# Choice of experts on one core: one-hot work for four heads at once, key rows for eight tokens, and fewer score and row buffers

## The chip, the cores and the metric

The kernel runs on one core of one Trainium2 chip. The metric is device time in microseconds (us) of one execution. In the profile PE is TensorE's matrix multiplication, PEld its weight load, DVE VectorE, ACT ScalarE, POOL GpSimd and SP the engine whose queue issues most DMAs.

## What is computed

One layer of a generator over 1024 latent tokens of width 1024: a mixer (state-space scan and a convolution group, with an output projection), then a retrieval of experts (PEER), then a final norm. The change lies in the retrieval. Each token has 8 heads. A head has two scores against 128 keys each; of each the 16 best are kept, the 16 best of their sums are chosen, and these give 16 of 16,384 experts with softmax gates:

```python
s = jnp.einsum("thpd,hpkd->thpk", q, sub_keys).astype(jnp.float32)
sv, si = lax.top_k(s, PEER_TOPK)
cand = sv[:, :, 0, :, None] + sv[:, :, 1, None, :]
best, flat = lax.top_k(cand.reshape(t, PEER_HEADS, PEER_TOPK * PEER_TOPK), PEER_TOPK)
i1 = jnp.take_along_axis(si[:, :, 0], flat // PEER_TOPK, axis=-1)
i2 = jnp.take_along_axis(si[:, :, 1], flat % PEER_TOPK, axis=-1)
experts = (i1 * N_KEYS + i2).reshape(t, PEER_HEADS * PEER_TOPK)
gates = jax.nn.softmax(best, axis=-1).reshape(t, PEER_HEADS * PEER_TOPK).astype(h.dtype)
act = jax.nn.gelu(jnp.einsum("pd,ped->pe", xb, u_tab[eb]), approximate=False)
out = jnp.einsum("pe,ped->pd", gb * act, v_tab[eb])
```

## The kernel before

**Stages.** The first 700 us or so are the mixer. Then comes the choice of experts for blocks 0 to 6 (a block is 128 tokens, one a partition). In the last stage the experts' work for blocks 0 to 4 is done densely (all 128 groups of 128 experts, L996 and L1443 to L1445, weighted by a gate matrix), while the experts of blocks 5 to 7 are fetched row by row by indirect DMAs (L1286) and worked off on DVE (L1311, L1323); the choice for block 7 runs within this stage, two heads at a time, paced by the matrix work (`advance`, L1357).

**One block's choice** is the generator `select` (L1022), with `nh` heads at once: 8 in the choice stage, 2 for block 7. For each head and each of its two scores DVE finds the 16 best values and their positions with five instructions (`top16`, L1030): values go to `v`, positions to `ix`. `ix` is read as float (L1057), the first key's position is scaled by 128 (L1058), and `stair` (L1037) forms the 50 candidate sums that can be among the best 16: the values on DVE, the key numbers on POOL (L1062), which reads `ixf`, the same memory as `ix`. A second `top16` over the candidates gives `best` and `pos` (L1080). Then the key number of each chosen place is looked up by one-hot work on DVE, head by head (L1084 to L1095): compare the position with a list of candidate positions, `lex` (L1089), multiply by the key numbers (L1091), sum (L1077, in `place`). The first 8 places need only 20 candidates, the other 8 all 50, so a head has two comparisons, two products and two sums over 8 x 20 = 160 and 8 x 50 = 400 elements. The sums of a head are put off until after the next head's products (`pend`). Last come the exponentials and the division (L1097 to L1105).

**The order is written out** by a clock. At each `yield` of `select` a cost is handed to `tick` (L1126), which adds it up and, per 1.0 of cost, takes one step of the oldest waiting work in `fill`, and, per 1.75, one step of `ahead`, the scores of coming blocks. A score phase (the first `top16`s) has 40 yields of 0.4, the rest of a block 19.2 of cost; a block has 35.2.

- `ahead` is `scores` (L1137). A score of a head pair (`score`, L949) is eight matmuls in four steps on TensorE, each record in the trace being half a matmul, and its eviction by ScalarE to a tile `s` comes with the next step (L959). `while len(SC) > 2` (L1143) holds the next one back while three scores lie ready. The scores of block 7 are made in between in blocks 1 and 2 and go to memory. After the scores, `prepare` (L1000) begins the last stage's matrix work.
- `fill` holds the gate matrices of blocks 0 to 4 (`gate_matrix`, L1174), four tokens a step, 32 steps with work and six more. `second` (L1208) builds on DVE a one-hot matrix `ob` of the second key, in 2-byte type, 512 elements a partition (L1211), and ScalarE scales it by the gates to `o2` (L1214); a step later `first` (L1217) builds on DVE `o1`, the first key's, in 4-byte type (L1219); a step later TensorE multiplies them (L1197); a step later ScalarE stores the product (L1204).

DVE, ScalarE and TensorE execute in this written order, each on its own. `tp2` (L1115) holds the tiles of the choice stage; a tile's `bufs` is how many copies take turns. `put` (L1169) gives the tiles of expert numbers `ef` and gates `gt`.

Of the kernel before, what the change touches and what calls it, by code (L numbers as in the profile page):

```python
# [8 lines left out]
F32 = mybir.dt.float32  # L9
F32R = mybir.dt.float32r  # L10
BF16 = mybir.dt.bfloat16
I32 = mybir.dt.int32
U32 = mybir.dt.uint32
AF = mybir.ActivationFunctionType
# [15 lines left out]
NH = 8  # L30
# [42 lines left out]
def layer_kernel(ctx, tc, A, dbg=None):  # L73
# [690 lines left out]
    def natural(blocks, ps, tp, name):  # L764

        for z, k4 in [(z, k4) for z in blocks for k4 in range(2)]:
# [3 lines left out]
            hn = tp.tile([P, 4, P], F32, name=name)  # L770
# [251 lines left out]
    def select(z, tp, nh, scores, put):  # L1022
# [23 lines left out]
        for h0 in range(0, NH, nh):  # L1046
# [20 lines left out]
            best = tp.tile([P, nh, TOPK], F32, name="best", bufs=1)  # L1067
            pos = tp.tile([P, nh, TOPK], U32, name="pos", bufs=1)
            posf = tp.tile([P, nh, TOPK], F32, name="posf", bufs=1)
            ef, gt = put(z, h0)  # L1070
            pend = []

            def place(n):
                while len(pend) > n:
                    q, oh = pend.pop(0)
                    for i, o in enumerate(oh):
                        nc.vector.tensor_reduce(ef[:, q, i * 8:i * 8 + 8], o, axis=mybir.AxisListType.X, op=OP.add)  # L1077

            for q2 in range(0, nh, 2):
# [3 lines left out]
                nc.vector.tensor_copy(posf[:, q2:q2 + 2], pos[:, q2:q2 + 2])  # L1083
                for q in (q2, q2 + 1):  # L1084
                    oh = tp.tile([P, 8, NUP + NCAND], F32, name="oh").rearrange("p a b -> p (a b)")
                    oh = [o.rearrange("p (a b) -> p a b", a=8) for o in (oh[:, :8 * NUP], oh[:, 8 * NUP:])]
                    for i, o in enumerate(oh):
                        sh = [P, 8, NCAND if i else NUP]
                        nc.vector.tensor_tensor(o, posf[:, q, i * 8:i * 8 + 8, None].to_broadcast(sh),  # L1089
                                                lex[:, None, :sh[2]].to_broadcast(sh), op=OP.is_equal)  # L1090
                        nc.vector.tensor_tensor(o, o, cand[:, 1, q, None, :sh[2]].to_broadcast(sh), op=OP.mult)  # L1091
                    pend.append((q, oh))
                    yield 0.7
                    place(nh // 8)
                    yield 0.7  # L1095
            eb = tp.tile([P, nh, TOPK], F32, name="eb", bufs=1)
            nc.vector.tensor_tensor(eb, best, best[:, :, 0:1].to_broadcast([P, nh, TOPK]), op=OP.subtract)  # L1097
            nc.scalar.activation(eb, eb, AF.Exp)
            yield 0.2
            place(0)  # L1100
            yield 0.9
# [12 lines left out]
    with ExitStack() as st:  # L1114
        tp2 = st.enter_context(tc.tile_pool(name="tp2", bufs=2))  # L1115
        spl = st.enter_context(tc.tile_pool(name="spl", bufs=4))
# [20 lines left out]
        def scores():  # L1137
# [3 lines left out]
            for z in range(NS):  # L1141
                for hh in range(4):
                    while len(SC) > 2:  # L1143
                        yield
# [486 lines left out]
```

## Time and profile before

| | us |
|---|---|
| median of three runs | 3053.84 |
| lowest, highest | 3052.66, 3054.78 |
| the profiled execution, its own time | 3052.06 |
| its span in the trace | 3050.3 |

Times are read from the trace of the profiled execution. A start is counted from the start of the span. The time between the starts of two instructions of one engine is what the first costs there when the engine doesn't wait; its length can be more, as the next may begin before it ends. In a row, `oh<-posf,lex 128x400` means the tile written, the tiles read, and partitions by elements; `x2` means two instructions shown as one. `[1.32 <-ACT s L959]` is idle time before the instruction and what ended it.

### The profile page before, as it was taken

Reading aid. Unit: us, or ns where it says so; the run is one execution under the profiler, and the core shown is the slowest. Engines: PE = TensorE matmul, PEld = TensorE weight load, DVE = VectorE, ACT = ScalarE, POOL = GpSimd, SP = SyncE. Lnnn points to the kernel's source line nnn. Section 1 sums busy time; section 2 is a strip of 40 time slices with the busy share of each in tenths; the row PEclk is TensorE's granted clock in tenths of the full one; section 3 lists DMA queues with packets and bytes.
Section 4 is the critical chain, followed back from the end, with each engine's and each line's share of the span. In section 5 each row is a group of like instructions: output and inputs, shape, how many; then the busy total and the mean of one; then the engine's idle time right before and its main releaser. Section 6 shows DMA issues by size and latency. Waiting matters only on the chain.

```text
span 3050.3 us, 41960 instructions
## 1 busy us (share of the span) xinstructions
PE 2836.3 (93%) x15129; PEld 2391.2 (78%) x15129; DVE 2570.6 (84%) x5084; ACT 1060.9 (35%) x2026; POOL 1326.0 (43%) x1043
## 2 busy tenths in 40 slices
PE   7999899998888876999999999999999999999996
PEld 3777698764555556898888998998998898998995
DVE  4898756659999999889989998888998888888886
ACT  3224333333667664332222222222222322322222
POOL 0212343420000002666566656566666566666650
PEclk8999899999999987999999999999999999999998
DMA  6211256250221235888889999998998998999993
GB/s 214 61 36 42 86 165 213 77 189 15 118 107 63 111 125 192 308 312 301 311 297 361 324 346 343 326 340 320 337 344 317 334 357 318 336 342 318 328 326 119
DMA packets 334545, 722.68 MB, mean 237 GB/s; under 512 B 24560, under 2 KB 167168, under 8 KB 333056
## 3 DMA queue, kind: packets, MB, share of 16 engines
q0 software_dynamic: 112176, 408.47, 37.1%
q1 hardware_dynamic: 222160, 311.53, 29.5%
q8 instruction: 119, 1.95, 0.2%
q14 instruction: 90, 0.74, 0.1%
HBM read 658.56 MB, written 61.35 MB: 236 GB/s over the span
## 4 chain that ended last, share of the span: by engine, by line
PE 58%; DVE 27%; issue 5%; DMA 5%; POOL 3%; ACT 2%; SPq 0%; DVEq 0%; POOLq 0%; ACTq 0%
PE pa L996 22%; PE pv L1444 8%; PE pv L1445 8%; PE pv L1443 8%; PE pa L68 4%; DVE o L1219 3%; DVE cfm L413 2%; DVE oh L1091 2%; DVE ob L1211 2%; POOL gr L1286 2%; DVE oh L1089 2%; DVE gr L1311 1%; DVE ef L1077 1%; PE pq L953 1%; PE po L68 1%
## 5 line engine op out<-in xcount | busy, mean ns | idle before, releaser
L1286 POOL DMA_INDIRECT gr<-in_peer_v_dram,idx x384 | 546.8, 1424 | 309.3 <-DVE h2T L1323 209.7
L1286 POOL DMA_INDIRECT gr<-in_peer_u_dram,idx x384 | 524.1, 1365 | 361.4 <-DVE gr L1311 249.2
L1444 PE MATMUL pv<-vl,wh 128*128 128x512 f32 x1240 | 495.5, 400 | 19.5 <-DVE vl L61 17.3
L1323 DVE SCALAR_TENSOR_TENSOR h2T<-gr,wv,h2T 128x1024 f32<-128x1024 f32 x381 | 488.5, 1282 | 13.6 <-DMA gr<-in_peer_v_dram,idx 6.0
L1443 PE MATMUL pv<-vh,wl 128*128 128x512 f32 x1240 | 493.4, 398 | 1.5 <-ACT vh L60 1.4
L1445 PE MATMUL pv<-vh,wh 128*128 128x512 f32 x1240 | 493.6, 398 | 0.0
L1311 DVE SCALAR_TENSOR_TENSOR gr<-gr,h2T 128x1024 f32<-128x1024 f32 x384 | 455.5, 1220 | 23.5 <-DMA gr<-in_peer_u_dram,idx 23.3
L60 ACT ACTIVATE vh<-v 128x512 fp32r<-128x512 f32 x256 | 161.5, 632 | 656.1 <-PE pv L1445 616.7
L996 PE MATMUL pa<-hh,ul 128*128 128x320 f32 x2000 | 335.0, 310 | 3.2 <-DVE ul L988 3.2
L996 PE MATMUL pa<-hh,uh 128*128 128x320 f32 x2000 | 334.6, 309 | 0.0
L996 PE MATMUL pa<-hl,uh 128*128 128x320 f32 x2000 | 334.0, 309 | 0.3 <-ACT ga L1406 0.3
L996 PEld LDWEIGHTS pa<-hl,uh 128*128 128x128 f32 x2000 | 304.8, 188 | 3.3 <-ACT ga L1406 0.6
L996 PEld LDWEIGHTS pa<-hh,ul 128*128 128x128 f32 x2000 | 304.2, 188 | 3.7 <-DVE ul L988 3.7
L996 PEld LDWEIGHTS pa<-hh,uh 128*128 128x128 f32 x2000 | 304.4, 188 | 0.0
L1444 PEld LDWEIGHTS pv<-vl,wh 128*128 128x128 f32 x1240 | 235.0, 190 | 80.0 <-DVE vl L61 22.8
L1406 ACT ACTIVATE ga<-pa 128x320 f32<-128x320 f32 x252 | 109.2, 436 | 525.2 <-PE pa L996 507.1
L1443 PEld LDWEIGHTS pv<-vh,wl 128*128 128x128 f32 x1240 | 235.1, 190 | 57.8 <-ACT vh L60 2.4
L61 DVE TENSOR_TENSOR vl<-v,vh 128x512 fp32r<-128x512 f32 x256 | 176.4, 690 | 122.5 <-ACT vh L60 114.9
L1445 PEld LDWEIGHTS pv<-vh,wh 128*128 128x128 f32 x1240 | 235.3, 190 | 56.1
L1197 PEld LDWEIGHTS pg<-o,o 128*128 128x128 f32 x1280 | 174.1, 207 | 128.2 <-ACT o L1214 109.2
L1197 PE MATMUL pg<-o,o 128*128 128x128 f32 x1280 | 188.0, 297 | 75.7 <-ACT o L1214 67.3
L1214 ACT ACTIVATE o<-ob,tr 128x128 f32<-128x128 bf16 x640 | 209.4, 399 | 96.4 <-DVE ob L1211 94.4
(344 smaller groups left out, 4241.5 us busy)
## 6 DMA issues: line engine op xcount, KB each, us to landing
v<-in_peer_v_dram SPq DMA_DIRECT2D x256, 256.0 KB
u<-in_peer_ut_dram SPq DMA_DIRECT2D x87, 512.0 KB
g_dram<-stg SPq DMA_DIRECT2D x10, 4096.0 KB
gm<-g_dram SPq DMA_DIRECT2D x64, 640.0 KB
h2T<-in_peer_ut_dram SPq DMA_DIRECT2D x41, 512.0 KB
ld<-in_ada_w_dram SPq DMA_DIRECT2D x24, 512.0 KB
w<-in_w_in_t_dram SPq DMA_DIRECT2D x21, 512.0 KB
raw<-in_ada_w_dram SPq DMA_DIRECT2D x8, 1024.0 KB
```

What stands on the lines that cost most here:

```text
L60: nc.scalar.activation(hi, src, AF.Copy)
L61: (eng or nc.vector).tensor_tensor(lo, src, hi.bitcast(F32), op=OP.subtract)
L68: nc.tensor.matmul(out, a(k)[i], b(k)[j], start=start and t == 0 and k == 0, stop=stop and t == 2 and k == n - 1)
L996: nc.tensor.matmul(pa[half], x[:, k], y[:, k, half * TH:half * TH + TH], start=t == 0 and k == 0, stop=t == 2 and k == KD - 1)
L1197: nc.tensor.matmul(pg[:, j], o2[:, j], o1[:, j], start=True, stop=True)
L1214: nc.scalar.activation(o2[:, j], ob[:, :, j], AF.Copy, scale=tr[:, 1, t4 * 4 + j:t4 * 4 + j + 1])
L1286: nc.gpsimd.indirect_dma_start(out=g, out_offset=None, in_=A[t], in_offset=bass.IndirectOffsetOnAxis(ap=idx[:, b, e:e + 1], axis=0))
L1311: nc.vector.scalar_tensor_tensor(g, g, 1.0, h2, op0=OP.mult, op1=OP.mult, accum_out=act[:, e:e + 1])
L1323: nc.vector.scalar_tensor_tensor(ac, g, wv[:, e:e + 1], ac, op0=OP.mult, op1=OP.add)
L1443: nc.tensor.matmul(Out.pv[t], wl[:, sl], self.vh, start=i == 0, stop=False)
L1444: nc.tensor.matmul(Out.pv[t], wh[:, sl], self.vl, start=False, stop=False)
L1445: nc.tensor.matmul(Out.pv[t], wh[:, sl], self.vh, start=False, stop=i == GE - 1)
```

## The change

Nine edits, all in the choice of experts:

1. The one-hot work is done after the second `top16` of all heads, for `w` = 4 heads at once (2 for block 7): comparison, product and sum over 4 x 8 x 20 = 640 or 4 x 8 x 50 = 1600 elements, with a yield after each, and one buffer `oh`.
2. All positions of a block are cast to float in one instruction, not per two heads.
3. `best` and the exponentials lie in `v`, `pos` and its float form in `ix`, in place of tiles of their own.
4. The exponentials are formed ahead of the one-hot work.
5. `ob` is built for eight tokens at once, in every second step, with 2 larger buffers instead of 3; `o2` has 3 buffers instead of 4.
6. `o1` is built for eight tokens at once, in every second step.
7. The score tiles have 3 buffers instead of 4, and `scores` holds the next one back while two lie ready.
8. `ef` and `gt` have 2 buffers instead of 3.
9. A tile of another helper that shares the name `o1` gets the same size.

```diff
--- before.py
+++ after.py
@@ -767,7 +767,7 @@
             pt = ps.tile([P, 4, P], F32, name="pt")
             for a in range(4):
                 nc.tensor.transpose(pt[:, a], h2T[:, k4 * 4 + a, z * P:(z + 1) * P], ident)
-            hn = tp.tile([P, 4, P], F32, name=name)
+            hn = tp.tile([P, 8 if name == "o1" else 4, P], F32, name=name)[:, :4]
             nc.scalar.activation(hn, pt, AF.Copy)
             nc.sync.dma_start(h2n_dram[(z - ND) * P:(z - ND + 1) * P, k4 * 512:k4 * 512 + 512],
                               hn.rearrange("p k t -> p (k t)"))
@@ -1064,41 +1064,31 @@
             yield 0.5
             stair(nc.vector, v, cand[:, 0], SUMS[3:], SUMS[:3])
             yield 0.5
-            best = tp.tile([P, nh, TOPK], F32, name="best", bufs=1)
-            pos = tp.tile([P, nh, TOPK], U32, name="pos", bufs=1)
-            posf = tp.tile([P, nh, TOPK], F32, name="posf", bufs=1)
+            best, eb = v[:, :, 0], v[:, :, 1]
+            pos, posf = ix[:, :, 0], ixf[:, :, 1]
             ef, gt = put(z, h0)
-            pend = []
-
-            def place(n):
-                while len(pend) > n:
-                    q, oh = pend.pop(0)
-                    for i, o in enumerate(oh):
-                        nc.vector.tensor_reduce(ef[:, q, i * 8:i * 8 + 8], o, axis=mybir.AxisListType.X, op=OP.add)
-
             for q2 in range(0, nh, 2):
                 for n in together([top16(best[:, q], pos[:, q], cand[:, 0, q], tp.tile([P, NCAND], F32, name="c2", bufs=2))
                                    for q in (q2, q2 + 1)]):
                     yield 0.12 * n
-                nc.vector.tensor_copy(posf[:, q2:q2 + 2], pos[:, q2:q2 + 2])
-                for q in (q2, q2 + 1):
-                    oh = tp.tile([P, 8, NUP + NCAND], F32, name="oh").rearrange("p a b -> p (a b)")
-                    oh = [o.rearrange("p (a b) -> p a b", a=8) for o in (oh[:, :8 * NUP], oh[:, 8 * NUP:])]
-                    for i, o in enumerate(oh):
-                        sh = [P, 8, NCAND if i else NUP]
-                        nc.vector.tensor_tensor(o, posf[:, q, i * 8:i * 8 + 8, None].to_broadcast(sh),
-                                                lex[:, None, :sh[2]].to_broadcast(sh), op=OP.is_equal)
-                        nc.vector.tensor_tensor(o, o, cand[:, 1, q, None, :sh[2]].to_broadcast(sh), op=OP.mult)
-                    pend.append((q, oh))
-                    yield 0.7
-                    place(nh // 8)
-                    yield 0.7
-            eb = tp.tile([P, nh, TOPK], F32, name="eb", bufs=1)
+            nc.vector.tensor_copy(posf, pos)
             nc.vector.tensor_tensor(eb, best, best[:, :, 0:1].to_broadcast([P, nh, TOPK]), op=OP.subtract)
             nc.scalar.activation(eb, eb, AF.Exp)
-            yield 0.2
-            place(0)
-            yield 0.9
+            yield 1.1
+            w = min(nh, 4)
+            for q, i in [(q, i) for q in range(0, nh, w) for i in range(2)]:
+                sh = [P, w, 8, NCAND if i else NUP]
+                oh = tp.tile([P, w * 8 * NCAND], F32, name="oh", bufs=1)[:, :w * 8 * sh[3]]
+                oh = oh.rearrange("p (w a b) -> p w a b", w=w, a=8)
+                nc.vector.tensor_tensor(oh, posf[:, q:q + w, i * 8:i * 8 + 8, None].to_broadcast(sh),
+                                        lex[:, None, None, :sh[3]].to_broadcast(sh), op=OP.is_equal)
+                yield 0.2 * w
+                nc.vector.tensor_tensor(oh, oh, cand[:, 1, q:q + w, None, :sh[3]].to_broadcast(sh), op=OP.mult)
+                yield 0.2 * w
+                nc.vector.tensor_reduce(ef[:, q:q + w, i * 8:i * 8 + 8], oh, axis=mybir.AxisListType.X, op=OP.add)
+                yield 0.3 * w
             sm = tp.tile([P, nh], F32, name="sm")
             nc.vector.tensor_reduce(sm, eb, axis=mybir.AxisListType.X, op=OP.add)
             nc.vector.reciprocal(sm, sm)
@@ -1113,7 +1103,7 @@
     with ExitStack() as st:
         tp2 = st.enter_context(tc.tile_pool(name="tp2", bufs=2))
-        spl = st.enter_context(tc.tile_pool(name="spl", bufs=4))
+        spl = st.enter_context(tc.tile_pool(name="spl", bufs=3))
         gst = st.enter_context(tc.tile_pool(name="gst", bufs=2))
         psT = st.enter_context(tc.tile_pool(name="psT", bufs=2, space=PSUM))
         psG = st.enter_context(tc.tile_pool(name="psG2", bufs=3, space=PSUM))
@@ -1140,7 +1130,7 @@
             extra = [(z, hh) for z in range(NS, NT) for hh in range(4)]
             for z in range(NS):
                 for hh in range(4):
-                    while len(SC) > 2:
+                    while len(SC) > 1:
                         yield
                     yield from begun.pop(0) if begun else score(z, hh)
                     if z and hh % 2 and extra:
@@ -1167,8 +1157,8 @@
         EG = {}
         def put(z, h0):
-            EG[z] = (tp2.tile([P, NH, TOPK], F32, name="ef", bufs=3),
-                     heads(gates[:, z - ND], 0, NH) if z >= ND else tp2.tile([P, NH, TOPK], F32, name="gt", bufs=3))
+            EG[z] = (tp2.tile([P, NH, TOPK], F32, name="ef"),
+                     heads(gates[:, z - ND], 0, NH) if z >= ND else tp2.tile([P, NH, TOPK], F32, name="gt"))
             return EG[z]
         def gate_matrix(z, ef, gt):
@@ -1206,19 +1196,25 @@
                     nc.sync.dma_start(g_dram[z, t4 // 16], stg[0])
             def second(t4):
-                ts = slice(t4 * 4, t4 * 4 + 4)
-                ob = tp2.tile([P, P, 4], BF16, name="ob", bufs=3)
-                nc.vector.tensor_tensor(ob, iotx, tb[:, None, ts].to_broadcast([P, P, 4]), op=OP.is_equal)
-                o2 = tp2.tile([P, 4, P], F32, name="o2", bufs=4)
+                if t4 % 2 == 0:
+                    ts = tb[:, t4 * 4:t4 * 4 + 8].rearrange("p (a b) -> p a b", b=4)
+                    second.ob = tp2.tile([P, 2, P, 4], BF16, name="ob")
+                    nc.vector.tensor_tensor(second.ob, iotx[:, None].to_broadcast([P, 2, P, 4]),
+                                            ts[:, :, None].to_broadcast([P, 2, P, 4]), op=OP.is_equal)
+                o2 = tp2.tile([P, 4, P], F32, name="o2", bufs=3)
                 for j in range(4):
-                    nc.scalar.activation(o2[:, j], ob[:, :, j], AF.Copy, scale=tr[:, 1, t4 * 4 + j:t4 * 4 + j + 1])
+                    nc.scalar.activation(o2[:, j], second.ob[:, t4 % 2, :, j], AF.Copy,
+                                         scale=tr[:, 1, t4 * 4 + j:t4 * 4 + j + 1])
                 return t4, o2
             def first(t4, o2):
-                o1 = tp2.tile([P, 4, P], F32, name="o1")
-                nc.vector.tensor_tensor(o1, iot[:, None].to_broadcast([P, 4, P]),
-                                        tr[:, 0, t4 * 4:t4 * 4 + 4, None].to_broadcast([P, 4, P]), op=OP.is_equal)
-                return t4, o1, o2
+                if t4 % 2 == 0:
+                    first.o1 = tp2.tile([P, 8, P], F32, name="o1")
+                    nc.vector.tensor_tensor(first.o1, iot[:, None].to_broadcast([P, 8, P]),
+                                            tr[:, 0, t4 * 4:t4 * 4 + 8, None].to_broadcast([P, 8, P]), op=OP.is_equal)
+                return t4, first.o1[:, t4 % 2 * 4:t4 % 2 * 4 + 4], o2
             stg = [None]
             got = [None] * 3
```

## Rows read from the trace of the kernel before

**Rows 1.** Stretches: length, us busy (instructions) of PE, PEld, DVE, ACT, POOL; clock; DMA.

```profile
1000.00:1100.00 100.00, 80.30 (x380) 55.78 (x381) 98.07 (x401) 67.86 (x192) 6.10 (x22) 0.90 0.21 90
...
1400.00:1500.00 100.00, 94.20 (x530) 85.64 (x529) 91.36 (x204) 28.70 (x46) 60.96 (x52) 0.98 0.87 310
...
1600.00:1700.00 100.00, 99.92 (x539) 88.69 (x539) 91.33 (x93) 26.21 (x42) 66.75 (x48) 1.00 0.96 353
```

**Rows 2.** Chain of waits from 735 to 1155 us, shares by line.

```profile
by line: DVE o L1219 22.3%; DVE ob L1211 12.5%; DVE oh L1091 8.6%; DVE oh L1089 7.6%; DVE ef L1077 6.7%; DVE ix L1032 5.9%; DVE scr L1033 5.7%; DVE ix L1035 5.6%; DVE v L1031 4.4%; DVE v L1034 4.2%; DVE pos L1035 1.8%; DVE pos L1032 1.8%; D
```

**Rows 3.** Who waited for whom, 700 to 1200 us: us, times, longest.

```profile
ACT o L1214 <- DVE ob L1211: 94.4, 93, 4.9
...
DVE v L1031 <- ACT s L959: 6.0, 4, 2.1
...
PE pv L996 <- DVE ul L988: 2.0, 1, 2.0
```

**Rows 4.** DVE's integer copy of the choices, its line and one of them (start, length).

```profile
L1107 DVE CAST idx<-ef x6: 174/176/221, 1124.4 to 1592.9; 128x32 int32<-128x32 f32 x4, 128x128 int32<-128x128 f32 x2
...
1200.04 0.22 DVE L1107 CAST idx<-ef 128x128 int32<-128x128 f32 x1
```

**Rows 5.** DVE in order of time, one head's one-hot work: start us, length us, operation.

```profile
1106.92 0.33 DVE L1089 TENSOR_TENSOR oh<-posf,lex 128x160 f32<-128x160 f32 x1
1107.28 0.33 DVE L1091 TENSOR_TENSOR oh<-oh,cand 128x160 f32<-128x160 f32 x1
1107.53 0.57 DVE L1089 TENSOR_TENSOR oh<-posf,lex 128x400 f32<-128x400 f32 x1
1108.13 0.57 DVE L1091 TENSOR_TENSOR oh<-oh,cand 128x400 f32<-128x400 f32 x1
1108.62 0.42 DVE L1211 TENSOR_TENSOR ob<-iotx,tb 128x512 bf16<-128x512 bf16 x1
1108.96 0.68 DVE L1219 TENSOR_TENSOR o<-iot,tr 128x512 f32<-128x512 f32 x1
1109.56 0.79 DVE L1077 TENSOR_REDUCE ef<-oh 128x8 f32<-128x160 f32 x2
1110.26 0.41 DVE L1211 TENSOR_TENSOR ob<-iotx,tb 128x512 bf16<-128x512 bf16 x1
```

**Rows 6.** DVE in order of time, a cast of positions and what follows.

```profile
1103.25 0.18 DVE L1083 CAST posf<-pos 128x32 f32<-128x32 uint32 x1
1103.46 0.33 DVE L1089 TENSOR_TENSOR oh<-posf,lex 128x160 f32<-128x160 f32 x1
```

**Rows 7.** DVE in order of time, the waits for scores in blocks 2 and 3.

```profile
827.66 0.49 DVE L1031 MAX8 v<-s 128x8 f32<-128x128 f32 x2 [1.32 <-ACT s L959]
...
915.33 0.49 DVE L1031 MAX8 v<-s 128x8 f32<-128x128 f32 x2 [1.32 <-ACT s L959]
```

**Rows 8.** TensorE in order of time: gate-matrix steps (8 records), a score step (4).

```profile
1055.57 1.13 PE L1197 MATMUL pg<-o,o 128*128 128x128 f32 x8 [0.47 <-ACT o L1214]
1056.53 1.88 PE L953 MATMUL pq<-m,h2T 128*128 128x512 f32 x4
1058.25 1.05 PE L1197 MATMUL pg<-o,o 128*128 128x128 f32 x8
```

**Rows 9.** DVE, the end of block 3's choice and of block 4's score phase.

```profile
970.28 0.28 DVE L1103 TENSOR_REDUCE sm<-eb 128x8 f32<-128x128 f32 x1
...
999.86 0.23 DVE L1058 TENSOR_SCALAR ix<-ix 128x128 f32<-128x128 f32 x1
```

**Rows 10.** POOL and DVE in order of time, around the first search of positions.

```profile
924.59 3.90 POOL L1041 TENSOR_TENSOR cand<-ix 128x64 f32<-128x64 f32 x11 [74.69 <-DVE ix L1058]
...
1080.30 2.49 POOL L1041 TENSOR_TENSOR cand<-ix 128x64 f32<-128x64 f32 x11 [76.45 <-DVE ix L1058]
...
1081.91 0.09 DVE L1032 MATCH_VALUE_LOAD pos<-best,cand 128x8 f32 x1
```

**Rows 11.** ScalarE in order of time, stores of two gate-matrix steps.

```profile
1099.72 0.57 ACT L1204 ACTIVATE stg<-pg 128x512 f32<-128x512 f32 x1
...
1101.38 0.58 ACT L1204 ACTIVATE stg<-pg 128x512 f32<-128x512 f32 x1
```

## The prediction

> **What bounds the kernel now.** I read the busy time by stretches first, because the change touches only the choice of experts and the gate matrices beside it, about a sixth of the span. In that stage VectorE (DVE) is busy 98% of the time, TensorE 80%, ScalarE 68% [rows 1]. A busy share alone doesn't say that an engine sets the end, so the chain of waits comes next: between 735 and 1155 us it runs almost wholly over DVE, and more than half of it lies in the lines that the change rewrites [rows 2]. The waits agree: DVE waited only 6.0 us for a score, while ScalarE waited 94.4 us for DVE's `ob` [rows 3]. At the stage's end TensorE waits for DVE's `ul`, and DVE turns to those right behind the last choice, at 1200.04 us [rows 3, 4]. So DVE time saved in this stage moves everything behind it forward by as much, as long as DVE stays the bound.
>
> **What the larger operations save.** Element counts stay; only fixed costs go. Start to start, a product that needs the comparison in front of it comes 0.36 us after 160 elements and 0.60 after 400, 1.0 ns an element and 0.20 us fixed; where the next instruction needs nothing from the one in front, it is 0.25 and 0.49, so 0.09 fixed [rows 5].
>
> One-hot work: a head takes 1.70 us for four operations and 0.70 for its two sums, 2.40 in all and 19.2 us for eight heads [rows 5]. Afterwards twelve operations do it: 3 x 8 x 8 x 70 = 13,440 elements, 13.4 us, plus twelve fixed parts. In blocks 1 to 5 a gate-matrix operation mostly stands between two of them (0.09 each, 1.1 us); in blocks 0 and 6 mostly not (0.20, 2.4 us). Saved: about 4.6 us in five blocks and 3.4 in two, 30 us. Four casts of positions become one: three times 0.21 us go [rows 6], the one left is 96 elements longer, so 0.5 us a block, 3.5 us.
>
> Gate matrices: 32 `ob` and 32 `o1` a block become 16 and 16, so 160 instructions go in five blocks. `ob` holds DVE 0.34 us and `o1` 0.60 for 512 elements; at 0.5 and 1.0 ns an element 0.08 and 0.09 are fixed [rows 5]. Taken at a little less, 0.075, since two points give the slope only roughly: 12 us. **DVE saves 45 us**, give or take 3 for the fixed parts.
>
> [...] The rows show 0.09 to 0.20 us fixed, because the next instruction starts before the last has ended (the 0.33 us product at 1107.28 is followed at 1107.53) [rows 5]. [...] I take the rows' value.
>
> **What it adds.** First, fewer scores ready. A block's score phase has 40 steps of 0.4, 16 units of the selection's clock; the scores ahead get one step per 1.75 units, and a score takes four steps and a fifth for its eviction. Before, three scores lie ready when a block begins, so only head pair 3 (needed at unit 12) must be made, ready at unit 8.75. Now two lie ready: pair 2 is finished at 8.75, needed at 8, and pair 3 needs ten steps by unit 12, which gives seven; the missing ones are issued at the last moment. In the kernel before, this happens only in blocks 2 and 3, which also make scores of block 7; DVE waited 1.3 us at each of three places (the first and the last of them in [rows 7]). Afterwards seven more places have no slack. Price from below: 7 x 1.3 = 9 us. From above: one step is 1.72 us of TensorE and one gate-matrix step 0.96 [rows 8]; ten steps and about nine gate-matrix steps are 25.8 us, and DVE gets there after 12/16 of a 29.6 us phase [rows 9] less 0.6 saved, at 21.6; with the eviction that is a wait of 4.8 us, six blocks 29, less the 3.9 there already: 25 us. Block 4, whose phase I took, is the shortest, so the others wait less: I take 15, nearer to the lower row.
>
> Second, positions now lie in the buffer of key indices, which POOL still reads. The first search of positions loads its keys at 1081.91; POOL's additions, started at 1080.30, end at 1082.79 [rows 10]. DVE would wait 0.9 us here with everything queued behind it. In other blocks gate-matrix operations come between, but POOL also takes up to 3.90 us [rows 10]. Bounds over seven blocks: 0 and 9 us; I take 4.
>
> At nothing: fewer `ob`, `o2`, `ef` and `gt` buffers. ScalarE's steps follow each other in 1.66 us [rows 11], while DVE needs 29.6 / 16 = 1.85 us a unit, thus a step, in that short phase [rows 9], and `ob` serves two steps, so ScalarE waits less. If TensorE fell two steps behind, three `o2` buffers would stop ScalarE and the score evictions behind it; that is inside the upper bound above. The exponentials move ahead of the one-hot work, which hides them. In the last stage (block 7, two heads at a time) DVE loses 24 instructions, but the work there is TensorE's (94% and later 100% busy [rows 1]): no gain. Each of its four groups has 26 steps instead of 25, so the two further gather buffers come about 4 x 3.9 = 16 us later (100 steps between 1200.04 and 1592.9 [rows 4]); at 6% idle TensorE that is below 1 us.
>
> **The sum:** 45 - 15 - 4 = 26 us less. The profiled execution took 3052.06 us, the median of the runs is 3053.84; 26 off the one is 3026, off the other 3028, and I give 3028. The case's own range: 48 - 9 - 0 = 39 at best, 42 - 25 - 9 = 8 at worst, 3015 to 3046.
>
> **The rivals.** Something below 0.2% (6 us) can't be told from no change.
> - *Forecast, 3028*, chance 0.72.
> - *The score phase becomes TensorE's* (0.11): every score then waits as in the upper bound, and the three-deep `o2` holds ScalarE back as well, some 3 us a block on top. 45 - 25 - 18 = 2 us less: 3052, no change. For it: TensorE is already 80% busy [rows 1], and most of a score is made in that phase. Against it: the three places that had no slack waited 1.3 us only.
> - *`ob` loses its double rate* (0.08): over a third dimension. 512 elements in 2-byte type hold DVE 0.34 us, as many in 4-byte type 0.60 [rows 5]. At one element a step a pair takes 1.02 + 0.08 instead of 0.59, 0.51 us more, 80 times: 41 us on the bound engine. 41 - 26 = 15 us more: 3069, slower. It decides as soon as a pair takes over 0.92 us. For it: nothing in the trace has this shape. Against it: the innermost run of four elements stays as it is. [...]
> - *Fixed costs larger than start to start shows* (0.09): 433 instructions go in seven blocks (36 and 3 in each, and 160), and if each frees all that its duration has above its elements (0.57 us for 400, at 1.0 ns, is 0.17 [rows 5]), 433 x 0.17 = 74 and 74 - 19 = 55 us less: 2999. Against it: DVE starts the next instruction earlier than that. [...]
>
> Faster by over 0.2% means below 3047.7: the forecast and the last rival, 0.81; the forecast's range ends below it. Within 0.2%: 0.11. Slower: 0.08. The range 3010 to 3050 holds the forecast's and some of the second case; left out are the slower case, the large gain and a tail, under 0.2.
>
> **What would show it.** Right: the double `ob` at 0.68 us (not 1.2), the one-hot operations at about 0.8 and 1.8 us, four of each a block; DVE waiting for scores some 20 us in all, mostly at pairs 2 and 3, and up to 1 us a block for POOL; the last choice ending near 1174 instead of 1200, and all behind it shifted by the same. Wrong: waits for scores of over 40 us, TensorE above 95% busy in the stage; or the stage shorter by 26 us and the end not, were the last stage bound by something that doesn't start with it.

## The result and the profile after

The changed kernel takes 3028.69 us, the median of four runs (3025.99 to 3033.13); the kernel before took 3053.25 beside it. The ratio is 0.9924, with a 95% interval of 0.991 to 0.9937: faster by 24.6 us. The forecast was 3028. Its size came out by two misses against each other, and the profile shows both: VectorE (DVE) saved more than forecast, and the start of the last stage gave some of it back.

In the times of the runs, 0.2% is 6 us. Runs of one kernel differ by that much and more, so what follows leans on the traces: when the last choice ends, and when TensorE reaches a certain matmul. The profiled execution took 3029.6 us (before: 3052.06).

First the stretches, as in [rows 1]: length, then busy us and instructions of PE, PEld, DVE, ACT and POOL, the granted clock, the DMA share and GB/s.

```profile
1000.00:1100.00 100.00, 77.29 (x400) 57.98 (x401) 95.84 (x285) 74.42 (x215) 2.53 (x11) 0.91 0.20 85
1400.00:1500.00 100.00, 95.08 (x543) 86.94 (x542) 90.93 (x195) 27.37 (x44) 61.11 (x53) 0.98 0.88 302
```

In the choice stage DVE has 285 instructions in 100 us instead of 401, and its share fell by two points: it now waits. TensorE did not become the bound there (77%).

The chain of waits (710 to 1130 us, shares by line) says so as well; it answers to [rows 2]:

```profile
by line: DVE o L1215 15.4%; PE pq L953 12.1%; PE pg L1187 9.2%; DVE ob L1203 8.4%; DVE oh L1088 7.3%; DVE oh L1085 7.1%; DVE ef L1090 6.4%; DVE ix L1032 5.5%; DVE ix L1035 4.9%; POOL cand L1041 3.8%; DVE v L1031 3.7%; DVE v L1034 3.5%; DVE 
```

TensorE's score and gate-matrix lines are in it with 21% and POOL's with 4%. Before, the lines at the head of the chain were all DVE's.

Next, DVE's groups by line and shape, 690 to 1180 us (count, busy us and mean ns of one, idle time before):

```profile
L1215 DVE TENSOR_TENSOR o<-iot,tr 128x1024 f32<-128x1024 f32 x80 | 97.3, 1216 | 0.0
L1203 DVE TENSOR_TENSOR ob<-iotx,tb 128x1024 bf16<-128x1024 bf16 x80 | 54.3, 679 | 0.0
...
L1085 DVE TENSOR_TENSOR oh<-ix,lex 128x1600 f32<-128x1600 f32 x14 | 26.8, 1917 | 0.1
...
L1075 DVE CAST ix<-ix 128x128 f32<-128x128 uint32 x7 | 1.6, 226 | 0.2
```

The double `ob` lasts 679 ns, where half of it lasted 415 on average before: 0.52 ns for each further element, near the 0.5 of the prediction's estimate, so its rate is what it was. One cast a block is left, 226 ns.

Who waited for whom, 705 to 1168 us, against [rows 3]:

```profile
ACT o L1207 <- DVE ob L1203: 68.8, 53, 3.5
...
DVE v L1031 <- ACT s L959: 17.3, 10, 2.9
...
DVE ix L1032 <- POOL cand L1041: 3.5, 6, 0.8
```

DVE waits for a score at ten places, 17.3 us, and for POOL's key numbers in six blocks, 3.5 us. In the kernel before, from 705 us on, it waited for a score at three places:

```profile
DVE v L1031 <- ACT s L959: 3.9, 3, 1.3
```

The end of the last choice, in order of time, answers to [rows 4, 5]:

```profile
1158.46 0.82 DVE L1085 TENSOR_TENSOR oh<-ix,lex 128x640 f32<-128x640 f32 x1
1159.31 0.82 DVE L1088 TENSOR_TENSOR oh<-oh,cand 128x640 f32<-128x640 f32 x1
1160.17 0.82 DVE L1090 TENSOR_REDUCE ef<-oh 128x32 f32<-128x640 f32 x1
1161.03 1.82 DVE L1085 TENSOR_TENSOR oh<-ix,lex 128x1600 f32<-128x1600 f32 x1
1162.77 1.22 DVE L988 TENSOR_TENSOR ul<-u,uh 128x1024 fp32r<-128x1024 f32 x1
1163.91 1.82 DVE L1088 TENSOR_TENSOR oh<-oh,cand 128x1600 f32<-128x1600 f32 x1
1165.76 1.82 DVE L1090 TENSOR_REDUCE ef<-oh 128x32 f32<-128x1600 f32 x1
...
1168.25 0.22 DVE L1097 CAST idx<-ef 128x128 int32<-128x128 f32 x1
```

Six operations do what 24 did for four heads. The last copy of the choices starts at 1168.25 instead of 1200.04 us: the choice stage is 31.8 us shorter. But TensorE gained less from it. The 190th matmul into `pv`, a fixed point early in the last stage, starts at 1246.90 us after the change and at 1271.46 before, 24.6 earlier, and the last one 23.3 earlier. So some 7 us were lost between the last choice and TensorE's work behind it. The time from the end of the last choice to that 190th matmul is called the handover below: 71.2 us before the change, 78.4 after it.

SP's queue shows where. Before the change (start us, time to the last issue of the group, what is loaded):

```profile
1190.94 0.33 SPq L978 DMA_DIRECT2D u<-in_peer_ut_dram  x1
...
1192.31 5.90 SPq L1385 DMA_DIRECT2D gm<-g_dram  x2
1198.68 7.79 SPq L1428 DMA_DIRECT2D v<-in_peer_v_dram  x5
1206.53 0.42 SPq L978 DMA_DIRECT2D u<-in_peer_ut_dram  x1
```

and after it:

```profile
1164.01 0.33 SPq L978 DMA_DIRECT2D u<-in_peer_ut_dram  x1
...
1168.39 1.99 SPq L1381 DMA_DIRECT2D gm<-g_dram  x2
1170.43 9.78 SPq L1424 DMA_DIRECT2D v<-in_peer_v_dram  x5
1180.26 0.42 SPq L978 DMA_DIRECT2D u<-in_peer_ut_dram  x1
```

The first load of a gate matrix (`gm`) went out 7.9 us ahead of the choice's end; now it goes out 0.1 us ahead, because its memory lies on `v` and `ix`, which the change keeps in use to the end of the choice (the exponentials in `v`, the positions in `ix`); the experiments with tiles of their own, below, bear this out. The `v` and `u` loads stand behind it in the queue. The `u` that left 6.3 us behind the last choice now leaves 11.8 us behind it, and TensorE meets that:

```profile
1183.36 1.34 PE L996 MATMUL pa<-hh,uh 128*128 128x320 f32 x8
1187.44 2.50 PE L996 MATMUL pa<-hl,uh 128*128 128x320 f32 x8 [2.75 <-ACT uh L984]
1189.74 1.82 PE L996 MATMUL pa<-hh,ul 128*128 128x320 f32 x8
1191.40 1.33 PE L996 MATMUL pa<-hh,uh 128*128 128x320 f32 x8
```

It waits 2.75 us for `uh`, and the two groups behind the wait take 2.50 and 1.82 us where others take 1.34. The kernel before has no such gap here. Five of the 7 us lie around this wait, between the 64th and the 127th matmul into `pv`; 1.4 lie ahead of it and 0.8 behind it.

### The profile page after: what moved, and what is told of

It reads as the page before. It is cut to its first block, busy times and chain, and to the rows that moved or that the text cites. A ratio compares the mean times of both kernels' runs of the same rounds, so it can differ in the third digit from the quotient of the medians.

```text
span 3027.8 us, 41488 instructions
## 1 busy us (share of the span) xinstructions
PE 2830.4 (93%) x15129; PEld 2389.9 (79%) x15129; DVE 2525.5 (83%) x4627; ACT 1054.2 (35%) x2026; POOL 1333.3 (44%) x1043
## 4 chain that ended last, share of the span: by engine, by line
PE 62%; DVE 23%; DMA 5%; issue 4%; POOL 3%; ACT 2%; SPq 0%; DVEq 0%; POOLq 0%; ACTq 0%
PE pa L996 23%; PE pv L1440 8%; PE pv L1441 8%; PE pv L1439 8%; DVE cfm L413 3%; PE pq L953 3%; PE pa L68 3%; DVE o L1215 2%; PE po L68 2%; PE pg L1187 1%; DVE gr L1307 1%; DMA gr<-in_peer_u_dram,idx 1%; DVE oh L1085 1%; DVE oh L1088 1%; DVE ob L1203 1%
## 5 line engine op out<-in xcount | busy, mean ns | idle before, releaser
L1041 POOL TENSOR_TENSOR cand<-ix 128x32 f32<-128x32 f32 (+6 forms) x121 | 49.3, 445 | 463.3 <-DVE ix L1058 463.3
L953 PE MATMUL pq<-m,h2T 128*128 128x512 f32 x512 | 238.9, 606 | 0.4 <-DMA m<-m_dram 0.4
```

The source lines that it names most:

```text
L953: nc.tensor.matmul(ps, h2T[:, k, z * P:(z + 1) * P], m[:, k, hh * 512:hh * 512 + 512], start=k == 0, stop=k == KD - 1)
```

## The experiments

Three theories were open. (1) The sum is right term by term: one-hot work, gate matrices, waits for scores. (2) Rivals: a term is worth more or less than its arithmetic says, or one wait only moves to another place. (3) The end of the choice is not passed on in full, because of the queue shown above. The kernel before was run beside each group: 3056.41 us (first four), 3057.0 (next four), 3054.75 (last four). A ratio is to those. A trace shows one execution, and in it the choice stage begins with DVE's first search of a score: at 678.7 us before the change, at 679.2 after it, and anywhere from 676.1 to 683.7 in the traces below. So where two traces are compared, the length of the choice stage counts, from there to the end of the last choice: 521.5 us before the change, 489.3 after it.

### Four tokens again: what the wider rows are worth

```diff
-                if t4 % 2 == 0:
-                    second.ob = tp2.tile([P, 2, P, 4], BF16, name="ob")
...
+                ob = tp2.tile([P, P, 4], BF16, name="ob", bufs=3)
...
-                    first.o1 = tp2.tile([P, 8, P], F32, name="o1")
...
+                o1 = tp2.tile([P, 4, P], F32, name="o1")
```

> The changed kernel with the one-hot rows (ob and o1) built for four tokens again, 160 more instructions on VectorE; all else as changed. By the theory (VectorE sets the stage's pace, and an instruction that is independent of the one in front costs 0.07 to 0.08 us beside its elements) the stage and the whole get 11 to 13 us longer: about 3041 us. Rival 1, the whole fixed part of an instruction's duration counts (0.17 us): 27 us longer, 3056. Rival 2, with so few scores ready TensorE sets the pace of the stage: at most 3 us longer, 3032.

3040.76 us, ratio 0.9954 (0.9942 to 0.9967). The last choice ends 10.8 us later than in the changed kernel:

```profile
1179.08 0.22 DVE L1097 CAST idx<-ef 128x128 int32<-128x128 f32 x1
```

The waits for scores and POOL were 3.4 us shorter and a new one, for a free `o` buffer, 1.8 us, so DVE's work itself grew by 10.8 + 3.4 - 1.8 = 12.4 us. Added up from start to start, `ob` and `o1` alone take 150.7 us instead of 138.7, 12.0 more. The term of 12 us stands.

### Head by head again: what the one-hot work is worth

```diff
-            w = min(nh, 4)
-            for q, i in [(q, i) for q in range(0, nh, w) for i in range(2)]:
...
+            pend = []
...
+            for q in range(nh):
...
+                pend.append((q, oh))
+                yield 0.7
+                place(nh // 8)
+                yield 0.7
+            place(0)
```

> The changed kernel with the one-hot work head by head as before (six operations a head, sums put off by one head), 36 more instructions a block; casts, buffers and scores as changed. Theory: 30 us longer (4.6 us in each of five blocks and 3.4 in two), about 3058 us. Rival 1 (0.17 us for each of 252 instructions): 43 us longer, 3072. Rival 2 (TensorE sets the pace): under 15 us longer, below 3044.

3054.01 us, ratio 0.9997 (0.9989 to 1.0006): without this part the change gains nothing that can be measured. Summed over seven blocks, the work behind the score phase is 31.4 us longer (288.8 against 257.4), and the last choice ends 33 us later:

```profile
1201.32 0.22 DVE L1106 CAST idx<-ef 128x128 int32<-128x128 f32 x1
```

The term of 30 us stands. The time, though, lost only some 22 us (0.9997 - 0.9924, 0.0073 of 3055; against the changed kernel's second runs below, 0.9907, it is 27, and either is uncertain by 5 to 7). TensorE runs 29.6 us behind the changed kernel at 1254 us, and 21.6 at 1640: 8 us came back within the last stage. This stretch of matrix work, the 190th to the 1009th matmul into `pv`, takes 393.6 us in the kernel before, 393.2 in the changed one and 385.0 here; 385 to 387 are also seen in the traces of two further kernels below, 391 to 394 in all others. TensorE's waits in this stretch add up to 11 to 12.5 us in these three traces, at a mean granted clock of 0.99, and to 12 to 16 us in the others, at 0.97 to 0.99. Each of the three is the shortest or second shortest execution of its kernel (here 3050.0 us, of eleven up to 3059.34), so the difference may belong to the execution and not to the edit. What sets it was not found.

### Three scores ready again

This one starts from the kernel with four tokens, whose smaller rows leave memory for a fourth score buffer.

```diff
-        spl = st.enter_context(tc.tile_pool(name="spl", bufs=3))
+        spl = st.enter_context(tc.tile_pool(name="spl", bufs=4))
...
-                    while len(SC) > 1:
+                    while len(SC) > 2:
```

> The kernel of e1 with three scores ready again (four score buffers); to be compared with e1. Theory: VectorE's waits for scores fall from about 17 us to about 4 and the time by as much, 13 us: about 3028 us. Rival: the waits only show that TensorE is full in this stage, so they turn up elsewhere: same as e1, within 3 us.

3028.51 us, ratio 0.9904 (0.989 to 0.9919), so 12.3 us below the kernel it starts from (0.0050 in ratios, 15 us, uncertain by about 6). DVE's waits, 700 to 1170 us, in the kernel it starts from and here:

```profile
DVE v L1031 <- ACT s L959: 17.2, 11, 2.8
...
DVE v L1031 <- ACT s L959: 6.0, 4, 2.1
DVE o L1209 <- PE pg L1187: 2.3, 4, 0.9
```

The waits for scores are the 6.0 us of [rows 3] again. The rival, that the waits move to the gate matrices, falls here but for about half a microsecond (1.8 there); a base further below shows more of it. The choice stage is 10.8 us shorter (490.1 against 500.9) and the handover 2.2. So the fewer score buffers cost 12 to 15 us, for which the forecast had 15.

### Moving the first tiles of the last stage

```diff
         ep2 = st.enter_context(tc.tile_pool(name="ep2", bufs=2, reuse_waits="tile"))
+        for _ in range(2):
+            for n, d, k in (("vh", F32R, 512), ("vl", F32R, 512), ("ga", F32, TD)):
+                ep2.tile([P, k], d, name=n)
```

> The changed kernel; in the last stage other tiles (vh, vl, ga) are put first in their pool, so that the first gate-matrix loads gm no longer lie on the memory of the tiles of the choice (v, ix) that now live to its end. Theory of the handover (the choice ends 31.8 us earlier, but TensorE is only 25.4 us earlier some 50 us later, because gm, v and u loads are issued behind the last choice): gm and v are issued some us before the last choice ends, TensorE has no wait of 2.8 us for u, and 4 to 6 us are gained, about 3024 us. Rival: the loads are bound by the transfers themselves, or other tiles hold them: no change, 3029 within 2 us.

3026.78 us, ratio 0.9905 (0.9889 to 0.9922). It tells nothing of the handover: `gm` came to lie on other tiles that are in use to the end (its load is released by the last copy of the choices), and left at 1168.22 us, as late as in the changed kernel. TensorE stood where it stood in the changed kernel at 1224 us. This is one of the two further kernels in whose trace the matrix work took 385 to 387 us later on; its runs lie between 3016.81 and 3035.53 us, and the traced one took 3017.55.

### The changed kernel again, and `gm` on memory that is free early

```diff
+        for n, d, sh, k in (("vh", F32R, [512], 2), ("gm", F32, [ND * 2, 2, P // 2], 2), ("ga", F32, [TD], 2),
+                            ("vl", F32R, [512], 2), ("act", F32, [P], 2), ("wv", F32, [P], 2), ("v", F32, [512], NV)):
+            for _ in range(k):
+                ep2.tile([P, *sh], d, name=n, bufs=k)
```

The first run has no edit; the second orders the tiles so that the first `gm` should lie on `o1`.

> The changed kernel itself, as the base for e6 to e8 on the same chip: 0.8% below the kernel before, the last choice ending some 32 us earlier and the matrix work of the last stage some 25 us earlier.

3030.99 us, ratio 0.9907 (0.9887 to 0.9928).

> The changed kernel with the last stage's tiles in another order in their pool: the first gate-matrix tile gm now lies on the rows o1, which are free once the gate matrices are done, and the v tiles on ob and o2 (in e4 gm had come to lie on cand, oh, ef and gt, which live to the end too). Theory of the handover: the first gm load no longer waits for VectorE, gm and v are issued 3 to 4 us earlier, TensorE's wait for u is gone, and 3 to 6 us are gained against e5. Rival: other things set the first 50 us of the last stage: no change within 2 us.

3028.76 us, ratio 0.9903 (0.9882 to 0.9925): 2.2 us less, inside the uncertainty. The trace decides. With the choice's last copy at 1170.64, `gm` leaves 3.1 us ahead of its end:

```profile
1167.78 4.22 SPq L1385 DMA_DIRECT2D gm<-g_dram  x2
1172.04 10.28 SPq L1428 DMA_DIRECT2D v<-in_peer_v_dram  x5
```

Yet the handover is 78.4 us, against 78.2 in the changed kernel's second trace, and TensorE waits as long as ever (waits of PE, 1150 to 1230 us):

```profile
PE pa L996 <- ACT uh L984: 3.1, 1, 3.1
```

So `gm`'s wait for the choice alone was not it. In front of `gm` stands the load of the next `u`, which waits until DVE has read the last one (`ul`). DVE does that between operations of the choice, 5.7 us ahead of the choice's end; before the change it was 10.6 us. And behind `gm` the `v` loads still left 1.2 us behind the end.

### Two faster kernels

The first builds only `ob` for eight tokens, and has three scores ready and tiles of its own for the exponentials and positions; the second keeps eight tokens for both, and does the one-hot work for two heads at a time, with three scores ready and tiles of its own for the exponentials and the positions as floats.

```diff
-            best, eb = v[:, :, 0], v[:, :, 1]
-            pos, posf = ix[:, :, 0], ixf[:, :, 1]
+            best = v[:, :, 0]
+            eb = tp.tile([P, nh, TOPK], F32, name="eb", bufs=1) if nh == NH else v[:, :, 1]
+            pos = tp.tile([P, nh, TOPK], U32, name="pos", bufs=1) if nh == NH else ix[:, :, 0]
+            posf = tp.tile([P, nh, TOPK], F32, name="posf", bufs=1) if nh == NH else ixf[:, :, 1]
```

and, in the second alone, where `pos` stays in `ix`:

```diff
-            w = min(nh, 4)
+            w = min(nh, 2)
```

> The changed kernel with o1 for four tokens again (80 more instructions), which frees memory for four score buffers with three scores ready, and for tiles of their own for the exponentials and positions. Theory: + 6 us for o1, - 13 for the waits for scores, - 3.5 for the waits for POOL, - 4 at the handover (gm's first load no longer behind v): 14 us less than e5. Rival (TensorE is full in this stage and takes what the waits give): 0 to 6 us more than e5.

3015.54 us, ratio 0.9873 (0.9853 to 0.9894): 15.5 us below the changed kernel's second runs in medians and 10.4 in ratios, uncertain by about 9. That fits the theory's 14, and the rival, no gain, falls.

> The changed kernel with the one-hot work for two heads at once (24 instead of 12 instructions a block), which frees memory for four score buffers with three scores ready, and for tiles of their own for the exponentials and the float positions; positions still in the key rows. Theory: + 11 us for the one-hot work, - 13 for the waits for scores, - 4 at the handover, the waits for POOL (3.5) stay: 6 us less than e5. Rival (TensorE is full): 8 to 12 us more than e5.

3023.2 us, ratio 0.9891 (0.987 to 0.9912), 7.8 us below in medians and 4.9 in ratios, uncertain by about 9. The rival, 8 to 12 us more, falls. This is the other kernel with 385 to 387 us of matrix work in its trace.

### Taking the two causes apart

A base with `o1` for four tokens (which frees the memory), and on it the own tiles, the three scores, and both; the edits are those shown.

> The changed kernel with the second factors (o1) built for four tokens again, nothing else; the base of this job. Only half of the gate's saving is undone, so about 5.5 us slower than the changed kernel, near 3034 us. The first matmul of the last stage that stands for the handover (the 190th into pv) is expected 78 us behind the end of the last choice, as in the changed kernel, and not 71 as in the kernel before.

3032.8 us, ratio 0.9929 (0.9915 to 0.9943). The handover is 78.7 us.

> The base with tiles of their own for the exponentials, the positions and their copies in fp32, so that the arrays of best values and positions no longer stay in use to the end of a choice. Theory: this gives back the handover as well as the wait for POOL, so the 190th matmul into pv is 71 to 72 us behind the last choice and the time falls by 7 + 3.5 = 9 to 11 us against the base. Rival: the handover is set by the place of one division of u among the longer vector operations of the last choice; then the 190th matmul stays 77 to 78 us behind, and the time falls by the 3.5 us of the wait for POOL alone, 2 to 5.

3030.06 us, ratio 0.992 (0.9906 to 0.9933): 2.7 us less, with about 6 of uncertainty, which is nearer to the rival. In the trace the wait for POOL is gone (3.0 us in the base), while the one for a free `o` buffer grew from 0.7 to 2.3 us, so the choice stage is 2.2 us shorter (492.8 against 494.9); the 190th matmul stands 76.2 us behind the last choice: neither 71 nor 78. The theory, that own tiles give the handover back, falls; they give back a third at most.

> The base with four score buffers and a choice that waits until three are ready. Theory: the waits for scores fall from some 17 us to 4 and the time by 12 to 13 us against the base; the handover stays at 76 to 78 us, as the three-score run at four rows had it. Rival: without the waits the division of u moves ahead and the handover comes back too; then 71 to 72 us, and the time falls by 18 or more.

3020.47 us, ratio 0.9884 (0.9869 to 0.9899): 13.7 us less in ratios, uncertain by about 6. The waits for scores are 5.8 us instead of 17.5, the handover is 77.5. That is the theory's size, and the rival, a handover of 71 to 72 us, falls. But here some of the waits did move to the gate matrices; the wait for a free `o` buffer was 0.7 us in the base and is now

```profile
DVE o L1213 <- PE pg L1187: 4.9, 5, 1.3
```

so the choice stage is only 8.6 us shorter (486.3 against 494.9), not the 11.7 by which the waits for scores fell.

> The base with both: the fastest kernel of the study run again. Theory (the two parts add up, as waits of different stretches): 20 to 24 us below the base, some 38 below the kernel before, near 3014 us. Rival (the two give the same time back, because either shortens the same chain): no more than 14 below the base.

3013.48 us, ratio 0.9866 (0.9851 to 0.9881): the fastest of the study, 41 us below the kernel before. In ratios it is 19.2 us below the base, uncertain by about 6, which leaves both the theory's 20 to 24 and the rival's 14 open. The traces speak for the theory: the choice stage is 16.2 us shorter than the base's (478.7 against 494.9) and the handover 4.6, 20.8 in all. (TensorE is 23 to 25 us ahead of the base throughout the last stage, but 3.2 of that is an earlier start of the choice stage in this execution.) DVE's waits in its choice stage, and SP's queue around its end (the last copy ends at 1156.70):

```profile
DVE v L1031 <- ACT s L959: 3.7, 3, 1.3
DVE o L1215 <- PE pg L1189: 1.4, 2, 0.9
```

```profile
1147.82 0.33 SPq L978 DMA_DIRECT2D u<-in_peer_ut_dram  x1
...
1149.23 6.40 SPq L1381 DMA_DIRECT2D gm<-g_dram  x2
1156.59 9.49 SPq L1424 DMA_DIRECT2D v<-in_peer_v_dram  x5
1166.14 0.42 SPq L978 DMA_DIRECT2D u<-in_peer_ut_dram  x1
```

The handover over all traces, in us from the end of the last choice (minus: ahead of it), behind the length of the choice stage. The columns are worked out from SP's, DVE's and TensorE's instructions in order of time. "Both, first run" is the first of the two faster kernels above, which is the same program as "both":

| kernel | choice stage | `u` in front of `gm` | first `gm` | first `v` | next `u` | 190th matmul |
|---|---|---|---|---|---|---|
| before | 521.5 | -9.3 | -7.9 | -1.6 | 6.3 | 71.2 |
| changed | 489.3 | -4.5 | -0.1 | 2.0 | 11.8 | 78.4 |
| changed, again | 490.8 | -4.5 | -0.1 | 1.9 | 11.8 | 78.2 |
| four tokens | 500.9 | -4.5 | -0.1 | 1.8 | 12.1 | 78.3 |
| head by head | 521.4 | -4.8 | -0.1 | 1.0 | 10.1 | 75.1 |
| four tokens, three scores | 490.1 | -8.9 | -0.1 | 1.4 | 10.6 | 76.1 |
| first tiles moved | 490.3 | -4.5 | 0.0 | 1.7 | 11.6 | 76.9 |
| `gm` on `o1` | 489.3 | -4.5 | -3.1 | 1.2 | 11.5 | 78.4 |
| base | 494.9 | -4.5 | -0.1 | 2.0 | 12.6 | 78.7 |
| base, own tiles | 492.8 | -4.5 | -3.1 | 1.5 | 11.6 | 76.2 |
| base, three scores | 486.3 | -8.9 | -0.1 | 1.0 | 10.4 | 77.5 |
| both | 478.7 | -8.9 | -7.5 | -0.1 | 9.4 | 74.1 |
| both, first run | 478.9 | -8.9 | -7.5 | -0.1 | 9.2 | 71.2 |
| two heads at a time | 493.2 | -10.0 | -8.5 | -5.4 | 6.0 | 72.0 |

On the whole, the later the next `u` leaves behind the choice, the later TensorE; and TensorE's wait for `uh` some 19 us behind the choice, 2.1 to 3.3 us, stands in every trace in which that `u` leaves 10.4 us or more behind the choice, and in none of the others. Two things hold the queue back. One is `gm`'s memory. The other is the `u` in front of it: it is released 4.5 to 4.8 us ahead of the end wherever two scores lie ready, with long operations or head by head, and 8.9 to 10.0 us wherever three do. (In the written order the last stage's first matrix work stands behind the scores in one list, so scores held back hold it back too; that is read from the code.) Either cure alone leaves the other to decide; with both the next `u` leaves 3 us earlier than in the base, and 4.6 and 7.5 us come back. That `u` is still 3 us later than before the change; what holds these back was not found. One kernel stood at 71.2 and 74.1 in its two profiled executions, so differences under 3 us are not to be read from the last column.

## Why the prediction was right

**That DVE is the bound, and stays it: right.** The choice stage became 31.8 us shorter, TensorE's share in it fell from 80% to 77% [rows 1], and the rival that makes the score phase TensorE's, with 25 us of waits for scores, did not come. One reading behind it was off, and it matters below: the 2.0 us for which TensorE waits for `ul` [rows 3] do not end behind the last choice but 9 us ahead of its end, with a `ul` that DVE makes between operations of the choice:

```profile
1190.97 1.80 PE L996 MATMUL pv<-hh,ul 128*128 128x320 f32 x8 [1.96 <-DVE ul L988]
```

**One-hot work, 30 us: right.** Done head by head again it costs 31.4. **Casts, 3.5:** not tested alone; three of four are gone and the one left takes 226 ns. Start to start, the casts of positions took 6.9 us before and take 1.0 after, so the term was too small by 2.4. **Gate matrices, 12: right.** With four tokens again 12.4 us of work came back. The double operations show it too: started one behind the other, in block 5,

```profile
1094.51 0.69 DVE L1203 TENSOR_TENSOR ob<-iotx,tb 128x1024 bf16<-128x1024 bf16 x1
1095.11 1.81 DVE L1090 TENSOR_REDUCE ef<-oh 128x32 f32<-128x1600 f32 x1
1096.84 1.22 DVE L1215 TENSOR_TENSOR o<-iot,tr 128x1024 f32<-128x1024 f32 x1
1097.98 0.28 DVE L1093 TENSOR_REDUCE sm<-v 128x8 f32<-128x128 f32 x1
```

the double `ob` holds DVE 0.60 us and the double `o1` 1.14, against twice 0.34 and twice 0.60 [rows 5]: 0.14 us for a pair, 11 us in 80. So `ob` kept its rate, and that rival fell.

**All in all DVE saves 45 +- 3: a little low.** The stage is 31.8 us shorter with 13.4 more us of waits for scores and 3.5 for POOL, so 48.7 us of work went. Added up by lines, start to start: one-hot work 139.4 us before and 109.6 after, `ob` and `o1` 149.8 and 138.7, casts of positions 6.9 and 1.0. That is 29.8 + 11.1 + 5.9 = 46.8; under 2 us lie in other lines. The rival of large fixed costs (74 us of work at 0.17 an instruction) falls: 48.7 us over 433 instructions is 0.11 each, between the 0.09 and 0.20 that starts show [rows 5]. That rival counted lengths, and a length can be more than an instruction costs: the `ob` above lasts 0.69 us and is followed after 0.60.

**Waits for scores, 15: right in places and price.** Ten places wait instead of three, the seven forecast; 13.4 us more. Three scores ready again takes 12 to 15 us off. The bounds 9 and 25 held. **POOL, 4: right**, 3.5 us.

**The exponentials ahead of the one-hot work and `best` in `v`, at nothing: this is the step that failed.** The prediction looked at these tiles' readers within the block and not at what lies on the same memory afterwards. Kept in use to the end of the last choice, `v` and `ix` hold back the first `gm` load. A second part belongs to the step on the fewer scores, which priced only DVE's waits: scores held back also put off DVE's `ul`, on which the queue waits in front of `gm`, by some 5 us relative to the end. So "all behind it shifted by the same" did not hold: the last choice ended almost 6 us earlier than the 1174 forecast, and TensorE gained 24.6 us of the 31.8. The net, 26, was nearly met by luck: the waits came out 2 us smaller, the saving 4 larger, and the handover took 7.

**The last stage at nothing: right.** Its choice, block 7's, ends with the copy at 1578.2 us instead of 1592.9 [rows 4], 14.7 us earlier, where TensorE is 25 earlier: so it lies 10 us later in the matrix work (forecast 16). TensorE kept its lead through it, 24.6 us at the 190th matmul, 25.0 at the 1009th; only in the last third did 2.4 us go.

## What to carry to other kernels

A tile put into another's memory to save space is in use longer: ask what lies on that memory in the next stage, and which queue its load holds up (here `gm` left 0.1 us ahead of the choice's end instead of 7.9); a change that shortens a stage is worth only what its handover lets through, here 24.6 us of 31.8. And giving back buffers on which an order written out by hand relies is dear: two scores ready instead of three cost nearly half of what the wider one-hot work brought, in waits (13.4 us against 29.8), and put off the next stage's first work as well. Restoring them, with tiles of their own, made the fastest kernel here, 3013.48 us.

## What the runs showed of the hardware

**More was lost at this wait of TensorE than its length.** Behind the 2.75 us wait at 1184.7 the granted clock is 0.50 from 1187.4 to 1189.5 us, 0.68 in the 2 us after it, and 1.00 again from 1191.5; that the wait lowered it is not shown (stretches of the changed kernel: PE, PEld, DVE, ACT, POOL, clock, DMA):

```profile
1180.00:1184.50 4.50, 4.32 (x29) 3.98 (x28) 2.39 (x3) 2.62 (x7) 0.00 (x0) 1.00 0.81 253
1187.40:1189.50 2.10, 2.06 (x8) 2.06 (x9) 2.08 (x8) 2.10 (x4) 0.00 (x0) 0.50 1.07 318
1189.50:1191.50 2.00, 2.00 (x11) 2.00 (x11) 2.00 (x4) 0.11 (x1) 0.53 (x1) 0.68 1.02 343
1191.50:1195.00 3.50, 3.50 (x26) 3.50 (x25) 3.50 (x7) 0.50 (x1) 2.89 (x3) 1.00 0.74 241
```

From the 64th to the 127th matmul into `pv` the changed kernel takes 52.0 us and the one before 47.0. Of the 5.0 us, 2.75 are the wait, and 1.6 lie in the two groups at a clock of 0.50 and 0.68, which take 2.30 and 1.66 us from start to start instead of 1.17; the rest lies in the steps beside them.

**A comparison and a product of DVE took longer beside POOL's subtractions.** In block 6 POOL computes `hl` (three operations) while DVE does the one-hot work. First DVE's two, then POOL's, in the changed kernel:

```profile
1149.70 3.17 DVE L1085 TENSOR_TENSOR oh<-ix,lex 128x1600 f32<-128x1600 f32 x1
1152.91 3.05 DVE L1088 TENSOR_TENSOR oh<-oh,cand 128x1600 f32<-128x1600 f32 x1
```

```profile
1147.14 7.14 POOL L61 TENSOR_TENSOR hl<-h2T,hh 128x640 fp32r<-128x640 f32 x3 [5.92 <-ACT hh L60]
```

They take 3.17 and 3.05 us, where the other two of this size in block 6, at 1161.03 and 1163.91 with no subtraction of POOL beside them, take 1.82. By single instructions, POOL's second and third end at 1151.19 and 1154.28, and DVE's two each 1.7 us behind one of these ends. The kernel before has the same on two operations over 160 elements, which take 1.63 and 1.47 us instead of 0.33; they end at 1170.14 and 1171.71, each 0.2 us behind one of POOL's, which end at 1169.95 and 1171.53. So the two engines' work side by side went with 2.6 us more on DVE in this block of the changed kernel; what holds DVE up there the traces do not show.
